# A fused transformer step: the seven products of halves are summed along chains in PSUM instead of on VectorE

## Chip, cores and metric

The kernel runs on one core of a Trainium2 chip. The metric is the device time of one execution in microseconds (us); shorter is better.

## What is computed

One step of a decoder layer for 2048 prompt tokens and 32 sample tokens, 1024 wide: a mixer (gated linear attention beside a spatial gating unit), a cross-attention over 256 memory tokens, and a gated feed-forward part with a causal convolution of width 3 (ConvFFN, 2816 wide). The two places that the change touches are these lines:

```python
q = (hn @ wq_x).reshape(B, T, MEM_HEADS, MEM_DH)
s = jnp.einsum('bthd,bmhd->bhtm', q, mk).astype(jnp.float32) * (MEM_DH ** -0.5)
p = jax.nn.softmax(s, axis=-1).astype(mv.dtype)
...
g = hn @ w_gate
gp = jnp.concatenate([buf.astype(g.dtype), g], axis=1)
c = conv_b + sum(conv_w[j] * gp[:, j:j + T] for j in range(CONV_W))
out = (jax.nn.gelu(c) * (hn @ w_up)) @ w_down
```

## The kernel before

The prompt runs in four blocks of 512 tokens, block 0 to 3; the 32 sample tokens ride along in the mixer of block 1 and in the ConvFFN of block 2, and their own cross-attention is spread over the ConvFFN of block 1 (its matmuls are `sop`, `soT`, `kTp`; its values are loaded as `vc`). Every fp32 product is three matmuls of rounded parts (`mm3`, L91 to L94: high by high, high by low, low by high). ScalarE (ACT) makes a high part and VectorE (DVE) the low one (`split`, L84 and L85).

Gate, up and the scores use a product of 2 x 2 halves with seven products instead of eight. The halves of a weight tile are A11, A12, A22 and the sums S1 to S4; the tokens are cut into halves of H = 256 (272 in block 2, with the sample tokens). One FFN step (`seven_step`) makes 256 columns of gate or up for a block: seven products of 4 x 3 = 12 matmuls. There are 11 gate and 11 up steps in each of the blocks 1 to 3; the very first gate step of each of these blocks takes another path (`early`). A score half-block (`sc{s}{i}`, two per block) is seven products of 24 matmuls. The names read as follows: `wup18S2` is block 1, up, step 8, half S2; `a_...` is the PSUM result, `r_q_...` the tile in SBUF with the four quarters q0 to q3 that the seven results add up to; `h_wup..` and `l_wup..` are the split parts of a loaded sum `r_wup..`. `g`, `c` and `acth` are the gate, its convolution and the product with up, `d` the down product.

Before, each product has a PSUM result of its own. With H = 256 ("joint" steps) S1 and S3 share a bank and S4 and A22 share one, at different columns. ScalarE copies A11 to q0 (L266); VectorE adds the other six results in: L268 (q3 = S2 + q0), L273 (q1 and q2 from S1, S3 and q3 in one instruction), L279 (q3 = S3 + q1), L258 (q0 += A12), L286 (q1 and q2 += S4 and A22); with H = 272 and in the scores each add is an instruction of its own. In the scores the copy is L1325, the adds are L1322, and `soften` (maximum, exponential, sum) follows for each quarter.

A scheduler of the framework sets each engine's order from the program and its own estimates, and takes PSUM results from two pools of four banks, `acc` and `mps`; neighbouring steps are interleaved by it. Accesses of two engines to one bank are kept apart with semaphores by it, whatever columns they touch. Each engine works through its queue strictly in order; the loads are issued from SyncE's queue (SPq). The input of the next block is loaded (L757) while the FFN still runs, and ScalarE squares it (`junk`, L758) for its norm.

## Time and profile before

| | |
|---|---|
| time, median of 3 runs | 2842.79 us (2840.3 to 2844.05) |
| span of the profiled execution | 2835.0 us |
| TensorE (PE) busy | 2794.4 us, 99% |
| VectorE (DVE) busy | 1891.3 us, 67% |
| ScalarE (ACT) busy | 1104.5 us, 39% |
| GpSimd (POOL) busy | 575.5 us, 20% |
| mean granted TensorE clock | 0.996 |
| DMA | 638.21 MB, 225 GB/s |

The span runs from the first to the last instruction of one execution taken with the profiler; the page gives no other time for that execution, and the median of the runs lies 7.8 us above its span. Busy times of different engines overlap. The ConvFFN stretches of the blocks 1, 2 and 3 are 1127 to 1484, 1818 to 2142 and 2483 to 2788 us of the span.

### The profile page before, as it was taken

Reading aid. Unit: us, or ns where it says so; the run is one execution under the profiler, and the core shown is the slowest. Engines: PE = TensorE matmul, PEld = TensorE weight load, DVE = VectorE, ACT = ScalarE, POOL = GpSimd, SP = SyncE. Lnnn points to the kernel's source line nnn. Section 1 sums busy time; section 2 is a strip of 40 time slices with the busy share of each in tenths; the row PEclk is TensorE's granted clock in tenths of the full one; section 3 lists DMA queues with packets and bytes.
Section 4 is the critical chain, followed back from the end, with each engine's and each line's share of the span. In section 5 each row is a group of like instructions: output and inputs, shape, how many; then the busy total and the mean of one; then the engine's idle time right before and its main releaser. Section 6 shows DMA issues by size and latency. Waiting matters only on the chain.

```text
span 2835.0 us, 47063 instructions
## 1 busy us (share of the span) xinstructions
PE 2794.4 (99%) x17894; PEld 2473.9 (87%) x17894; DVE 1891.3 (67%) x3266; ACT 1104.5 (39%) x1950; POOL 575.5 (20%) x638
## 2 busy tenths in 40 slices
PE   8999999999999999999999999999999999999998
PEld 8888888888888898898888889899999888899997
DVE  6578778777657776655555777766666677665555
ACT  5645544333363354222124445422223545421222
POOL 2002212111111221222220121222221022132222
PEclk9999999999999999999999999999999999999999
DMA  9756589999932255888995226577776323577775
GB/s 306 244 182 219 188 273 340 335 339 333 328 109 77 83 164 196 309 290 290 324 340 169 82 61 208 196 260 256 258 264 215 102 70 133 201 260 273 271 282 177
DMA packets 369687, 638.21 MB, mean 225 GB/s; under 512 B 27370, under 2 KB 238412, under 8 KB 369462
## 3 DMA queue, kind: packets, MB, share of 16 engines
q1 hardware_dynamic: 369462, 635.20, 65.9%
q8 instruction: 142, 2.33, 0.3%
q14 instruction: 83, 0.68, 0.1%
HBM read 507.69 MB, written 127.41 MB: 224 GB/s over the span
## 4 chain that ended last, share of the span: by engine, by line
PE 61%; DVE 4%; ACT 1%; issue 1%; POOL 1%; DMA 0%; POOLq 0%; SPq 0%; DVEq 0%; ACTq 0%
PE d L94 4%; PE d L92 4%; PE d L93 4%; PE a_wx L94 1%; PE a_wx L93 1%; PE a_wx L92 1%; PE s L1044 1%; PE a_wo L92 1%; PE a_wo L93 1%; PE a_wu L92 1%; PE a_wu L93 1%; PE a_wo L94 1%; PE t_wr L92 1%; PE t_wr L93 1%; PE a_wu L94 1%
## 5 line engine op out<-in xcount | busy, mean ns | idle before, releaser
L92 PE MATMUL d<-acth,whi_wd 128*128 128x272 f32 (+1 forms) x688 | 235.3, 342 | 0.0
L94 PE MATMUL d<-acth,wlo_wd 128*128 128x272 f32 (+1 forms) x688 | 233.3, 340 | 0.0
L93 PE MATMUL d<-actl,whi_wd 128*128 128x272 f32 (+1 forms) x688 | 233.0, 339 | 0.0
L1679 DVE TENSOR_TENSOR h<-d,h 128x512 f32<-128x512 f32 (+1 forms) x232 | 133.5, 581 | 148.0 <-PE d L94 147.8
L1581 POOL TENSOR_TENSOR c<-c,bc_f 128x512 f32<-128x512 f32 (+1 forms) x88 | 139.3, 1589 | 134.2 <-ACT c L1580 133.4
L1571 ACT ACTIVATE c<-g,colsb 128x512 f32<-128x512 f32 x88 | 71.7, 815 | 202.9 <-DVE g L1540 152.7
L94 PEld LDWEIGHTS d<-acth,wlo_wd 128*128 128x128 f32 x688 | 129.3, 188 | 15.5 <-issue 1.2
L93 PEld LDWEIGHTS d<-actl,whi_wd 128*128 128x128 f32 x688 | 129.3, 188 | 13.6 <-issue 0.4
L92 PEld LDWEIGHTS d<-acth,whi_wd 128*128 128x128 f32 x688 | 129.5, 188 | 13.1
L1603 POOL TENSOR_TENSOR c<-r_q_wup,c 128x512 f32<-128x512 f32 (+1 forms) x33 | 63.0, 1908 | 337.7 <-DVE r_q_wup L286 215.9
L1568 POOL COPY carry<-g 128x2 f32<-128x2 f32 x88 | 30.6, 348 | 432.8 <-DVE g L1540 430.7
L92 PE MATMUL a_wo<-ch,h_wo 128*128 128x512 f32 (+1 forms) x320 | 113.2, 365 | 2.3 <-ACT r L874 1.5
L93 PE MATMUL a_wo<-cl,h_wo 128*128 128x512 f32 (+1 forms) x320 | 113.4, 357 | 0.0
L94 PE MATMUL a_wo<-ch,l_wo 128*128 128x512 f32 (+1 forms) x320 | 112.6, 355 | 0.0
L1572 DVE SCALAR_TENSOR_TENSOR c<-g,colsb,c 128x512 f32<-128x512 f32 x88 | 86.0, 978 | 29.0 <-ACT c L1571 28.3
L84 ACT ACTIVATE acth<-c 128x512 fp32r<-128x512 f32 (+1 forms) x88 | 55.9, 636 | 117.1 <-DVE c L1603 87.3
L94 PE MATMUL a_wx<-pTh,wlo_wx 128*128 128x512 f32 x256 | 101.2, 395 | 0.0
L93 PE MATMUL a_wx<-pTl,whi_wx 128*128 128x512 f32 x256 | 100.5, 393 | 0.0
L92 PE MATMUL a_wx<-pTh,whi_wx 128*128 128x512 f32 x256 | 100.2, 394 | 0.0
L1580 ACT ACTIVATE c<-c 128x512 f32<-128x512 f32 (+1 forms) x88 | 56.1, 637 | 96.6 <-DVE c L1573 84.7
L1573 DVE SCALAR_TENSOR_TENSOR c<-g,colsb,c 128x512 f32<-128x512 f32 x88 | 88.0, 1000 | 1.1
L85 DVE TENSOR_TENSOR actl<-c,acth 128x512 fp32r<-128x512 f32 (+1 forms) x88 | 64.2, 733 | 27.2 <-ACT acth L84 26.2
(3753 smaller groups left out, 9725.5 us busy)
## 6 DMA issues: line engine op xcount, KB each, us to landing
whi_wd<-wd SPq DMA_DIRECT2D x66, 512.0 KB, 7.8
wlo_wd<-wd SPq DMA_DIRECT2D x66, 512.0 KB, 7.5
r_wo<-in_w_out_dram SPq DMA_DIRECT2D x32, 512.0 KB, 3.5
wlo_wx<-vod SPq DMA_DIRECT2D x32, 512.0 KB, 4.1
whi_wx<-vod SPq DMA_DIRECT2D x32, 512.0 KB, 4.8
r_wg<-in_w_gate_dram SPq DMA_DIRECT2D x22, 512.0 KB, 7.4
r_wup<-in_w_up_dram SPq DMA_DIRECT2D x22, 512.0 KB, 4.7
r_wd<-in_w_down_dram SPq DMA_DIRECT2D x22, 512.0 KB, 4.3
```

The source lines that it names most:

```text
L84: act.activation(hi, src, AF.Copy)
L85: (lo_eng or dve).tensor_tensor(lo, src, hi.bitcast(F32), ALU.subtract)
L92: pe.matmul(ps, wh, xh, start=first, stop=False)
L93: pe.matmul(ps, wh, xl, start=False, stop=False)
L94: pe.matmul(ps, wl, xh, start=False, stop=last)
L1571: act.activation(c[:, :SB], g[:, 2:SB + 2], AF.Identity, bias=cb, scale=w2)
L1572: dve.scalar_tensor_tensor(c[:, :SB], g[:, 1:SB + 1], w1, c[:, :SB], ALU.mult, ALU.add)
L1573: dve.scalar_tensor_tensor(c[:, :SB], g[:, 0:SB], w0, c[:, :SB], ALU.mult, ALU.add)
L1580: act.activation(c[:, :T], c[:, :T], AF.Gelu_apprx_tanh)
L1581: pool.tensor_tensor(c[:, :T], c[:, :T], B.fbc[:, :T], ALU.mult)
L1603: (dve, pool)[i].tensor_tensor(c[:, :T], q[i], c[:, :T], ALU.mult)
L1679: dve.tensor_tensor(B.h[m + mm][:, cs], ps[:, :cw], B.h[m + mm][:, cs], ALU.add)
```

## The change

The four chains x (A11, S2, S3), y (S1, S4), z (A12) and w (A22) each get one PSUM result, and a product is added onto its chain by TensorE. The running sums are copied out by ScalarE: A11 to q0, A11+S2 to q1, A22 to q2, S1 to q3. VectorE then adds x onto q2 and q3 once (after S3), and z and y onto q0 and q1 once (after S4). In joint steps x and w share one bank, and z and y another; A22 and A12 start there without the flag that starts a sum, since another sum is open in the bank. The order of products becomes A11, S1, A12, S2, A22, S3, S4. The number of matmuls stays the same. The first gate step of a block (`early`) computes as before.

```diff
@@ mm3
-    def mm3(ps, wh, wl, xh, xl, first, last):
-        pe.matmul(ps, wh, xh, start=first, stop=False)
...
+    def mm3(ps, wh, wl, xh, xl, first, last, again=False):
+        pe.matmul(ps, wh, xh, start=first, stop=False, skip_group_check=again)
...
+    CHAIN = {"A11": "x", "S2": "x", "S3": "x", "S1": "y", "S4": "y", "A12": "z", "A22": "w"}
+    COPIED = {"A11": 0, "S2": 1, "A22": 2, "S1": 3}
@@ seven_step
-        seq = ("A11", "S1", "A12", "S2", "S3", "S4", "A22") if early else ("A11", "S2", "S1", "S3", "A12", "S4", "A22")
-        joint = 2 * H <= 512 and not early
+        seq = ("A11", "S1", "A12", "S2", "S3", "S4", "A22") if early else ("A11", "S1", "A12", "S2", "A22", "S3", "S4")
+        joint = 2 * H <= 512
...
-                if nm == "A11":
-                    act.activation(q0, got(nm), AF.Copy)
-                elif nm == "S2":
-                    dve.tensor_tensor(q3, got(nm), q0, ALU.add)
...
-                elif nm == "S3":
-                    if joint:
-                        dve.tensor_tensor(q[:, H:3 * H].rearrange("p (s t) -> p s t", s=2),
-                                          ps[nm][0].rearrange("p (s t) -> p s t", s=2),
-                                          q3.unsqueeze(1).broadcast_to([128, 2, H]), ALU.add)
-                    else:
-                        dve.tensor_tensor(q1, got("S1"), q3, ALU.add)
-                        dve.tensor_tensor(q2, got(nm), q3, ALU.add)
-                    dve.tensor_tensor(q3, got(nm), q1, ALU.add)
-                elif nm == "A12" and not early:
-                    c11()
-                elif nm == "S4" and not joint:
-                    dve.tensor_tensor(q1, got(nm), q1, ALU.add)
-                elif nm == "A22":
-                    if joint:
-                        dve.tensor_tensor(q[:, H:3 * H], ps[nm][0], q[:, H:3 * H], ALU.add)
-                    else:
-                        dve.tensor_tensor(q2, got(nm), q2, ALU.add)
+                if joint:
+                    xw, zy = acc(f"a_{name}x"), acc(f"a_{name}z")
+                    at_ = {"x": xw[:, :H], "w": xw[:, H:2 * H], "z": zy[:, :H], "y": zy[:, H:2 * H]}
+                else:
+                    at_ = {i: acc(f"a_{name}{i}")[:, :H] for i in "xyzw"}
+                q23 = q[:, 2 * H:4 * H].rearrange("p (s t) -> p s t", s=2)
+                for nm in seq:
+                    i = CHAIN[nm]
+                    fresh = nm in ("A11", "S1") or not joint and nm in ("A12", "A22")
+                    for k in range(last + 1):
+                        mm(at_[i], nm, k, fresh and k == 0, k == last)
+                    if nm in COPIED:
+                        act.activation(q[:, COPIED[nm] * H:(COPIED[nm] + 1) * H], at_[i], AF.Copy)
+                    elif nm == "A12" and not joint:
+                        dve.tensor_tensor(q0, at_["z"], q0, ALU.add)
+                    elif nm == "S3":
+                        dve.tensor_tensor(q23, at_["x"].unsqueeze(1).broadcast_to([128, 2, H]), q23, ALU.add)
+                    elif nm == "S4" and joint:
+                        dve.tensor_tensor(q[:, 0:2 * H], zy[:, 0:2 * H], q[:, 0:2 * H], ALU.add)
+                    elif nm == "S4":
+                        dve.tensor_tensor(q1, at_["y"], q1, ALU.add)
@@ score
-        SEQ = ("A11", "S1", "A12", "S2", "S3", "S4", "A22")
+        SEQ = ("A11", "S1", "A12", "S2", "A22", "S3", "S4")
...
-                ps = B.ps[nm] = acc(f"sc{s}{i}{nm}")
+                fresh = nm in ("A11", "S1", "A12", "A22")
+                if fresh:
+                    B.ps[CHAIN[nm]] = acc(f"sc{s}{i}{nm}")
+                ps = B.ps[CHAIN[nm]]
...
+                if nm in COPIED:
+                    o = COPIED[nm]
+                    q[o] = T_(f"p{s}{i}{o}")
+                    act.activation(q[o][:, :512], ps, AF.Copy)
+                for o in {"A12": (0,), "S3": (3, 2), "S4": (1,)}.get(nm, ()):
+                    dve.tensor_tensor(q[o][:, :512], ps, q[o][:, :512], ALU.add)
+                    soften(i, o)
```

Two places show how the order moves; both are up 8 and gate 9 of block 1 (`wup18`, `wg19`), where the next block's input (`x2_00` and so on) is squared. First ScalarE's queue, before the change (L266 are the copies of A11):

```order
L84 ACTIVATE h_wup18S2_14539<-r_wup18S2_14537 128x1024
L1580 ACTIVATE c117_14653<-c117_14653 128x512
L84 ACTIVATE h_wup18S1_14665<-r_wup18S1_14663 128x1024
L266 ACTIVATE r_q_wup18_14856<-a_wup18A11_14857 128x256
L758 ACTIVATE junk_90,xss2_15569<-x2_00_15579 128x512
L758 ACTIVATE junk_90,xss2_15569<-x2_01_15582 128x512
L84 ACTIVATE h_wup19S2_14973<-r_wup19S2_14971 128x1024
L758 ACTIVATE junk_90,xss2_15569<-x2_10_15585 128x512
L84 ACTIVATE acth116_14953<-c116_14643 128x512
L758 ACTIVATE junk_90,xss2_15569<-x2_11_15588 128x512
L266 ACTIVATE r_q_wg19_14985<-a_wg19A11_14986 128x256
```

And with the change, where the copies have the line L280 (the rows of up 8 are in turn S1, A11+S2 and, behind two squares and an `acth`, A22; those of gate 9 A11 and S1):

```order
L280 ACTIVATE r_q_wup18_14796<-a_wup18z_14798 128x256
L280 ACTIVATE r_q_wup18_14796<-a_wup18x_14797 128x256
L758 ACTIVATE junk_90,xss2_15494<-x2_00_15504 128x512
L84 ACTIVATE acth116_14890<-c116_14583 128x512
L758 ACTIVATE junk_90,xss2_15494<-x2_01_15507 128x512
L280 ACTIVATE r_q_wup18_14796<-a_wup18x_14797 128x256
L758 ACTIVATE junk_90,xss2_15494<-x2_10_15510 128x512
L84 ACTIVATE h_wup19S1_14910<-r_wup19S1_14908 128x1024
L280 ACTIVATE r_q_wg19_14922<-a_wg19x_14923 128x256
L280 ACTIVATE r_q_wg19_14922<-a_wg19z_14924 128x256
L758 ACTIVATE junk_90,xss2_15494<-x2_11_15513 128x512
L280 ACTIVATE r_q_wg19_14922<-a_wg19x_14923 128x256
```

Before, one copy per step stands here, gate 9's behind four squares. Now three copies stand between the squares: up 8's last one behind `x2_01`, gate 9's first two behind `x2_10` and `h_wup19S1`.

Second, TensorE at the end of up 8, before the change (the last matmuls of A22, a step of the sample's output, and gate 9's A11):

```order
L92 MATMUL a_wup18S4_14926<-wuhwx17_11533,wup18A22_14755 128x256
L93 MATMUL a_wup18S4_14926<-wulwx17_11534,wup18A22_14755 128x256
L94 MATMUL a_wup18S4_14926<-wuhwx17_11533,wup18A22_14755 128x256
L1404 MATMUL sop0_14964<-r_so00_14757,sos_14835 32x256 x4
L92 MATMUL a_wg19A11_14986<-w1wx11_11275,wg19A11_14795 128x256
L93 MATMUL a_wg19A11_14986<-w1wx11_11275,wg19A11_14795 128x256
```

And with the change, from the last matmuls of A22 to the first of S3 of up 8 (`h_wup18S1` holds S1 and S3):

```order
L92 MATMUL a_wup18x_14797<-wuhwx17_11521,wup18A22_14695 128x256
L93 MATMUL a_wup18x_14797<-wulwx17_11522,wup18A22_14695 128x256
L94 MATMUL a_wup18x_14797<-wuhwx17_11521,wup18A22_14695 128x256
L1394 MATMUL sop0_14901<-r_so00_14697,sos_14775 32x256 x4
L92 MATMUL a_wg19z_14924<-wthwx17_11512,wg19S1_14782 128x256
L93 MATMUL a_wg19z_14924<-wtlwx17_11513,wg19S1_14782 128x256
L94 MATMUL a_wg19z_14924<-wthwx17_11512,wg19S1_14782 128x256
L1394 MATMUL sop0_14901<-r_so01_14794,sos_14775 32x256 x4
L1394 MATMUL sop0_14901<-r_so10_14899,sos_14775 32x256 x4
L92 MATMUL a_wup18x_14797<-wthwx11_11267,h_wup18S1_14482 128x256
L93 MATMUL a_wup18x_14797<-wtlwx11_11268,h_wup18S1_14482 128x256
L94 MATMUL a_wup18x_14797<-wthwx11_11267,l_wup18S1_14483 128x256
```

Behind A22 came a new step and nothing of up 8 any more; now only the sample's output and the end of gate 9's S1 lie between A22 and S3, which is added onto x in the bank that A22 shares, and so after A22's copy.

More of the change, by code (lines that the diff above doesn't have):

```diff
@@ L89, in split_scaled @@
         dve.scalar_tensor_tensor(lo, src, g, hi.bitcast(F32), ALU.mult, ALU.subtract)
-    def mm3(ps, wh, wl, xh, xl, first, last):
-        pe.matmul(ps, wh, xh, start=first, stop=False)
-        pe.matmul(ps, wh, xl, start=False, stop=False)
-        pe.matmul(ps, wl, xh, start=False, stop=last)
+    def mm3(ps, wh, wl, xh, xl, first, last, again=False):
+        pe.matmul(ps, wh, xh, start=first, stop=False, skip_group_check=again)
+        pe.matmul(ps, wh, xl, start=False, stop=False, skip_group_check=again)
+        pe.matmul(ps, wl, xh, start=False, stop=last, skip_group_check=again)
     def wraw(name):
@@ L240, in fn @@
             q0, q1, q2, q3 = (q[:, i * H:(i + 1) * H] for i in range(4))
-            ps = {}
-            def prod(nm, k0, k1):
-                if nm not in ps:
-                    mate = {"S3": "S1", "A22": "S4"}.get(nm)
-                    if joint and mate:
-                        ps[nm] = ps[mate][0], 1
-                    else:
-                        ps[nm] = (mps if early and len(ps) > 3 else acc)(f"a_{name}{nm}"), 0
-                bank, i = ps[nm]
-                for k in range(k0, k1):
-                    mm3(bank[:, i * H:(i + 1) * H], half(nm, 0, k), half(nm, 1, k), *xs[k][nm], k == 0, k == last)
@@ L254, in got, with mm @@
-            def got(nm):
-                return ps[nm][0][:, ps[nm][1] * H:(ps[nm][1] + 1) * H]
-            def c11():
-                dve.tensor_tensor(q0, got("A12"), q0, ALU.add)
+            def mm(bank, nm, k, first, stop):
+                mm3(bank, half(nm, 0, k), half(nm, 1, k), *xs[k][nm], first, stop, not early)
             if early:
+                ps = {nm: (mps if i > 3 else acc)(f"a_{name}{nm}")[:, :H] for i, nm in enumerate(seq)}
                 for nm in seq:
-                    prod(nm, 0, last)
@@ new lines, in fn @@
+                    for k in range(last):
+                        mm(ps[nm], nm, k, k == 0, False)
+                for nm in seq:
+                    mm(ps[nm], nm, last, False, True)
+                    if nm == "A11":
+                        act.activation(q0, ps[nm], AF.Copy)
+                    elif nm == "S2":
+                        dve.tensor_tensor(q3, ps[nm], q0, ALU.add)
+                        dve.tensor_tensor(q0, ps["A12"], q0, ALU.add)
+                    elif nm == "S3":
+                        dve.tensor_tensor(q1, ps["S1"], q3, ALU.add)
+                        dve.tensor_tensor(q2, ps[nm], q3, ALU.add)
+                        dve.tensor_tensor(q3, ps[nm], q1, ALU.add)
+                    elif nm == "S4":
+                        dve.tensor_tensor(q1, ps[nm], q1, ALU.add)
+                    elif nm == "A22":
+                        dve.tensor_tensor(q2, ps[nm], q2, ALU.add)
+            else:
+                if joint:
+                    xw, zy = acc(f"a_{name}x"), acc(f"a_{name}z")
+                    at_ = {"x": xw[:, :H], "w": xw[:, H:2 * H], "z": zy[:, :H], "y": zy[:, H:2 * H]}
+                else:
+                    at_ = {i: acc(f"a_{name}{i}")[:, :H] for i in "xyzw"}
+                q23 = q[:, 2 * H:4 * H].rearrange("p (s t) -> p s t", s=2)
+                for nm in seq:
+                    i = CHAIN[nm]
[6 more added lines that the diff above has]
+                        dve.tensor_tensor(q0, at_["z"], q0, ALU.add)
+                    elif nm == "S3":
+                        dve.tensor_tensor(q23, at_["x"].unsqueeze(1).broadcast_to([128, 2, H]), q23, ALU.add)
+                    elif nm == "S4" and joint:
+                        dve.tensor_tensor(q[:, 0:2 * H], zy[:, 0:2 * H], q[:, 0:2 * H], ALU.add)
+                    elif nm == "S4":
+                        dve.tensor_tensor(q1, at_["y"], q1, ALU.add)
@@ L1319, in fn @@
                         xh, xl = B.hn[k][nm]
[L1320 removed]
+                        mm3(ps[:, c * 256:(c + 1) * 256], xh[:, cs], xl[:, cs], wh[:, k], wl[:, k],
+                            fresh and c == 0 and k == 0, k == 3, True)
                 q = B.p[i]
[L1322 to L1342 removed]
+                if nm in COPIED:
[5 more added lines that the diff above has]
+                    soften(i, o)
             def load():
```

27 lines of the change are left out of this document (removed).

## Prediction

> **What bounds the kernel now.** I read the page's busy shares first, then a table of the stages that the change touches, then the waits of TensorE.
>
> ```profile
> span 2835.0 us, 47063 instructions
> PE 2794.4 (99%) x17894; PEld 2473.9 (87%) x17894; DVE 1891.3 (67%) x3266; ACT 1104.5 (39%) x1950; POOL 575.5 (20%) x638
> ```
>
> TensorE (PE) is busy for 2794.4 of 2835.0 us, so a time can only fall by fewer or shorter matmuls, or by closing what little idle time there is. The table by stage has, per row, the stretch, its length, the busy time of PE, PEld, DVE, ACT and POOL (instructions in brackets), the granted TensorE clock, the DMA share and GB/s. The first three rows are the ConvFFN of blocks 1, 2 and 3, the next two the scores of blocks 0 and 1.
>
> ```profile
> 1127.00:1484.00 357.00, 356.16 (x2753) 316.91 (x2753) 196.09 (x284) 91.22 (x141) 92.63 (x104) 1.00 0.86 307
> 1818.00:2142.00 324.00, 323.79 (x2582) 323.37 (x2582) 212.50 (x388) 85.52 (x141) 87.61 (x136) 1.00 0.73 258
> 2483.00:2788.00 305.00, 304.74 (x2218) 287.64 (x2218) 177.02 (x261) 74.28 (x111) 83.83 (x88) 1.00 0.77 273
> 324.00:367.00 43.00, 42.90 (x363) 42.70 (x362) 33.22 (x68) 22.63 (x48) 3.87 (x3) 1.00 0.78 265
> 1024.00:1074.00 50.00, 46.81 (x370) 45.38 (x369) 39.35 (x85) 25.69 (x55) 9.24 (x5) 0.97 0.64 218
> ```
>
> In these five stretches TensorE is idle for 0.84, 0.21, 0.26, 0.10 and 3.19 us, 4.6 us together. VectorE (DVE) is busy for 55 to 66% of the FFN stretches and 77 to 79% of the scores; it is not the bound. ScalarE (ACT) is busy for 24 to 26% and 51 to 53%. The waits of TensorE name what ended its idle time (total us, times, longest):
>
> ```profile
> PE otp L1185 <- DVE o L1179: 6.1, 3, 2.9
> PE sc10S L92 <- DVE h L1238: 1.7, 1, 1.7
> PE sop L1495 <- DMA vc<-in_cache_mem_v_dram: 0.5, 1, 0.5
> ```
>
> None of them is an add of a product of halves: the first is in the mixer, the second waits for the normalised input of the scores, the third for sample values from memory. What the change speeds up is therefore not waited for today.
>
> **The change, part by part: matmuls.** Every product keeps its 12 matmuls of 256 columns (272 in block 2) or its 24 in the scores. Adding into a sum that is already in PSUM instead of a fresh result alters only a flag. The first matmuls of two consecutive products of gate 6 in block 3 give the pace:
>
> ```profile
> 2643.83 0.28 PE L92 MATMUL a_wg36A<-w1wx,wg36A 128*128 128x256 f32 x1
> 2644.19 0.28 PE L92 MATMUL a_wg36S<-wuhwx,wg36S 128*128 128x256 f32 x1
> 2645.61 0.28 PE L92 MATMUL a_wg36S<-wthwx,wg36S 128*128 128x256 f32 x1
> ```
>
> From the first row of S2 (2644.19) to the first of S1 (2645.61) are 12 matmuls, 1.42 us, 0.118 us each. All but the first matmul of each product accumulate already, at the same pace. I take 0 us for the flag. No row shows a product that adds onto another product's sum; from the bracketing rows (first matmul of a product and those behind it, both 0.28 us) both ends are 0.
>
> **VectorE.** One gate step of block 1 adds five times now; the scores of one half-block add seven times (count, then duration min/median/max in ns):
>
> ```profile
> L268 DVE TENSOR_TENSOR r_q_wg<-a_wg12S,r_q_wg x1: 417/417/417, 1171.6 to 1171.6; 128x256 f32<-128x256 f32 x1
> L273 DVE TENSOR_TENSOR r_q_wg<-a_wg12S,r_q_wg x1: 692/692/692, 1174.3 to 1174.3; 128x512 f32<-128x512 f32 x1
> L258 DVE TENSOR_TENSOR r_q_wg<-a_wg12A,r_q_wg x1: 425/425/425, 1177.4 to 1177.4; 128x256 f32<-128x256 f32 x1
> L286 DVE TENSOR_TENSOR r_q_wg<-a_wg12S,r_q_wg x1: 692/692/692, 1180.3 to 1180.3; 128x512 f32<-128x512 f32 x1
> L1322 DVE TENSOR_TENSOR p<-sc00S,p x5: 681/683/691, 336.8 to 342.5; 128x512 f32<-128x512 f32 x5
> L1322 DVE TENSOR_TENSOR p<-sc00A,p x2: 681/686/691, 337.5 to 345.5; 128x512 f32<-128x512 f32 x2
> ```
>
> The fifth (L279) has the size of L268. So a joint step costs 3 x 0.42 + 2 x 0.69 = 2.64 us and will cost two adds of 512, 1.38: 1.26 less in each of 42 steps, 53 us. Block 2 goes from seven adds of about 0.43 to two of them and a double one, about 1.4 less in 21 steps, 29 us. Scores lose 3 x 0.69 in 8 half-blocks, 17 us. Some 99 us of VectorE's 1891 go. TensorE waits for none of it, so its worth is bounded by the idle time of the stretches above: 0 to -4.6 us, and the 0.03 of clock that the 50 us scores stretch lacks, 1.5 us. The one big wait there (sc10S, 1.7) is for L1238, ahead of the adds; I take 0.
>
> **ScalarE.** It copies four sums instead of one in 63 FFN steps (three of the 66 copies below belong to the first gate, which stays) and in 8 half-blocks.
>
> ```profile
> 0.00:2835.00 2835.00, 25.46 (x66) 1.00 0.66 225
> L1325 ACT ACTIVATE p<-sc00A x1: 572/572/572, 330.0 to 330.0; 128x512 f32<-128x512 f32 x1
> ```
>
> The first row is ACT's busy time in today's copies (L266): 25.46/66 = 0.386 us each. 189 more cost 73 us, 24 score copies at 0.57 another 14: 87 us on an engine that is busy for 1104.5. That is hidden as work. But a copy is now something that TensorE waits for: S2 may not be added onto A11's bank before A11 is copied out, nor may the other half of that bank be written meanwhile.
>
> The time that a copy has is set by what the order puts between a product and the one that needs its copy. The scheduler interleaves neighbouring steps, so in blocks 1 and 3 this is mostly two products, 2 x 1.42 = 2.8 us, at the tightest usually one (1.42); the scores have at least one product of 24 matmuls, 2.8. In need are 0.39 for the copy plus its start:
>
> ```profile
> 2644.45 0.39 ACT L266 ACTIVATE r_q_wg<-a_wg36A 128x256 f32<-128x256 f32 x1 [4.70 <-PE a_wg36A L94]
> ```
>
> A11's last matmul began just ahead of 2644.19, the copy stood ready and ended at 2644.84. So 0.65 us of 1.42 to 2.8 are used when ScalarE is free, and it may come 0.8 to 2.2 us late at no cost. For this hiding the price is 0 at one end, and at the other the lateness beyond it.
>
> The Trainium skill, "PSUM — Partial Sum Buffer", section "PSUM bank collisions raise a hardware error", speaks against the change: two engines must be kept off a bank as a whole, not off an address in it, so that a copy of one half shuts TensorE out of the other half too. By it each bank has up to four hand-overs a step; this order of products is laid out with such waits, and today's trace, in which no bank changes hands between ScalarE and TensorE within a step, cannot show the price. It is rival two.
>
> **Where ScalarE is late.** ScalarE takes its work strictly in order; what stands ahead of a copy decides. The one place where a slow thing stands there is gate/up 8 and 9 of block 1, in which the squares of the next block's input (`junk`, L758) wait for loads, which wait for the buffers of the last sample values. Today:
>
> ```profile
> 1426.06 1.63 SPq L757 DMA_DIRECT2D x<-in_x_prompt_dram  x3
> 1425.06 0.64 PE L1495 MATMUL sop<-vc,spm 128*32 128x256 f32 x8
> 1426.54 0.64 PE L1495 MATMUL sop<-vc,spm 128*32 128x256 f32 x8 [0.52 <-DMA vc<-in_cache_mem_v_dram]
> 1419.47 1.76 SPq L1437 DMA_DIRECT2D vc<-in_cache_mem_v_dram  x4
> 1434.28 0.64 PE L1404 MATMUL sop<-r_so,sos 128*32 128x256 f32 x8
> 1434.86 0.63 ACT L758 ACTIVATE junk<-x 128x512 bf16<-128x512 f32 x1 [11.08 <-DMA x<-in_x_prompt_dram]
> 1435.61 0.63 ACT L758 ACTIVATE junk<-x 128x512 bf16<-128x512 f32 x1
> 1436.24 1.04 ACT L84 ACTIVATE h_wup19S<-r_wup19S 128x1024 fp32r<-128x1024 f32 x1
> 1438.94 0.36 ACT L266 ACTIVATE r_q_wg<-a_wg19A 128x256 f32<-128x256 f32 x1
> ```
>
> ScalarE stood for 11.08 us, and nobody minded: only gate 9's copy came late, and it has no taker on TensorE. Call T0 the end of the last `sop` (1427.2): the load issues at T0-1.1, the first square starts at T0+7.7. In the new order up 8's copy of A22 stands behind two squares and an `acth`, and S3 of up 8 waits for it. ScalarE: T0+7.7, square 0.75, `acth` 0.53, square 0.63, so the copy runs from T0+9.6 to T0+10.0. TensorE: between T0 and S3 stand 59 matmuls of halves, 7.0 us, and three groups of the sample's output (L1404, 0.57 from the start of one to the next matmul in the trace), 1.7 us, so it is ready at T0+8.7. Stall 1.3. S3 ends near T0+11.4; gate 9's S2 then needs its A11 copy, which stands behind another square and `h_wup19S`: T0+9.9, plus 0.63, plus 1.0, plus 0.39 is T0+11.9, a stall of 0.5. Before that, the last `sop` comes nearer to its load: from the earlier `sop` to it were 5.6 us, in the new order some 4.9, so the 0.52 of waiting becomes about 1.1, 0.6 more. Together 2.4. The ends are 0 (the load lands 2 us sooner) and 5 (2 to 3 us later, with DMA at 86%).
>
> A stall of this size also costs clock. Behind the two long `otp` waits and the sc10S wait the granted clock (third figure from the right) read:
>
> ```profile
> 1026.00:1030.00 4.00, 2.29 (x10) 1.86 (x11) 4.00 (x10) 1.82 (x3) 1.05 (x2) 0.82 0.44 133
> 1030.00:1034.00 4.00, 3.58 (x21) 3.18 (x19) 3.96 (x8) 3.40 (x8) 1.12 (x1) 0.75 0.09 15
> 1684.00:1688.00 4.00, 3.09 (x9) 2.30 (x10) 2.68 (x5) 2.42 (x4) 0.00 (x0) 0.50 0.43 131
> 1688.00:1692.00 4.00, 4.00 (x14) 3.16 (x13) 0.73 (x2) 0.00 (x0) 0.00 (x0) 0.66 0.01 4
> ```
>
> After the 1.7 us wait 4 x 0.18 + 4 x 0.25 = 1.7 us were lost, after the 2.9 us one 4 x 0.50 + 4 x 0.34 = 3.4. I take 1.7, the row nearest to a stall of 1.3; the ends are 0 and 3.4. The Trainium skill, "TensorE: Matmul & The Clock Gate", section "Why this matters for your kernels", would have only gaps over some 3 us lower the clock; the rows above differ with waits of 1.7 and 2.9, and by the page the sum would be 1.7 less.
>
> **Sum.** Matmuls 0, VectorE 0, place at up 8 +2.4, clock +1.7, small lateness of copies elsewhere +0.5 (between 0 and 3; several `h_wup` splits that wait for memory stand ahead of copies in block 1). +4.6 on the span: 2839.6. The three runs' median, 2842.8, lies 7.8 above the profiled span, so 2847.4.
>
> **Rivals.** *One, nothing is felt*: the loads land early enough and all copies stay hidden, 2842 to 2844. For it: only one place has a slow thing ahead. Against it: the 11.08.
>
> *Two, every step stalls*: hand-overs of a bank cost TensorE time even with ScalarE free. If each of 42 joint steps lost 0.65 us once (the copy of gate 6, uncovered), +27; at four times, +109. It decides wherever less than 0.65 us of other products stands in between; against it, the order has 1.42 and more. Likeliest price if it holds in part: 2860 to 2950.
>
> *Three, block 1 stalls at several places*: the splits that wait for memory (`h_wup`) precede copies at gates 1, 7, 10 as well. Today's waits of ScalarE there:
>
> ```profile
> ACT h_wup17S L84 <- DMA r_wup17S<-s7u: 8.1, 1, 8.1
> ```
>
> Two more stalls like the one at up 8, each 1.3 and 1.7 of clock, give +3.0 apiece: one or two of them beside the whole of the forecast, 2850 to 2854, three or four 2856 to 2860.
>
> *Four, faster*: VectorE's 99 us end the scores of block 1 sooner and shift the mixer's work, so that one `otp` wait of 2.9 with its 3.4 us of clock goes: 2843 - 6.3 = 2836.5. It decides once VectorE reaches L1179 3 us sooner; against it, that line belongs to the mixer, ahead of any changed add of its block.
>
> **How the numbers follow.** The forecast, 2845 to 2851, gets 0.42, two thirds of it within 0.2% (5.7 us, about what a measurement of this kernel tells from no change); rival one 0.22; two 0.06; three 0.23; four 0.07. So faster 0.07, same 0.28 + 0.22 = 0.50, slower 0.14 + 0.06 + 0.23 = 0.43. The range 2838 to 2858 leaves out four, two and the tail of three. Without the rare cases it would be 2842 to 2853.
>
> **What would show it.** In the changed trace the waits of TensorE should name one or two `a_wup18x`/`a_wg19x` rows released by ScalarE's copy, 1 to 3 us, with a clock below 1.00 just behind; FFN stretches of blocks 2 and 3 should keep their idle time of 0.2 to 0.3; DVE should read about 1790 and ACT about 1190. Rows such as `a_wg3…x <- ACT` by the dozen would show rival two. It is wrong if the loads of the next input do not land as today, or if ScalarE lags elsewhere by more than 2 us.

## The result, and the profile after

The changed kernel takes 2849.41 us, the median of six runs (2848.23 to 2854.78); the kernel before, in six runs, 2840.27 (2840.04 to 2844.05). The ratio is 1.0036, its 95% interval 1.0026 to 1.0046, which is 7.4 to 13.1 us more. The profiled execution of the changed kernel is the slowest of its six, 2854.78 us, and the one of before a quick one, so the two spans are 18.1 us apart, twice the 9.1 us between the medians; what the waits shown here cost is therefore more than the usual price, and a second profile of the same kernel, at 2849.3 us, stands further below.

The head of the page of the changed kernel:

```profile
span 2853.1 us, 46922 instructions
PE 2801.9 (98%) x17894; PEld 2479.9 (87%) x17894; DVE 1796.5 (63%) x3032; ACT 1181.5 (41%) x2163; POOL 561.7 (20%) x638
```

VectorE lost 95 us of work and ScalarE gained 77. TensorE has the same number of matmuls. The table by stage, with the ConvFFN of blocks 1, 2 and 3 (columns as before):

```profile
1127.00:1490.00 363.00, 354.56 (x2697) 314.34 (x2696) 163.30 (x220) 110.02 (x200) 85.59 (x102) 0.99 0.83 292
1818.00:2160.00 342.00, 341.55 (x2684) 339.58 (x2683) 197.78 (x319) 115.80 (x215) 96.72 (x140) 1.00 0.73 254
2483.00:2808.00 325.00, 322.15 (x2299) 301.64 (x2298) 157.08 (x212) 104.13 (x184) 76.62 (x91) 1.00 0.75 264
```

The idle time of TensorE, length less busy time, is now 8.4 us in block 1 (0.8 before), 0.5 in block 2 (0.2) and 2.9 in block 3 (0.3). The stretches do not hold quite the same work as before: over the whole of block 3, from its gate 0 to the end of the span, the idle time is 12.5 us against 10.5. Even so the loss is in blocks 1 and 3, where two chains share a bank, and not in block 2. Which waits they are, from TensorE's waits (total us, times, longest; rows selected); the first two stand for what the change left as it was:

```profile
PE otp L1185 <- DVE o L1179: 5.9, 3, 2.9
PE sc10S L92 <- DVE h L1238: 1.6, 1, 1.6
...
PE d L92 <- DMA whi_wd<-wd: 6.1, 2, 3.4
PE a_wg36z L92 <- DMA wg36S<-s7g: 0.9, 1, 0.9
PE d L92 <- DVE r_q_wg L286: 0.8, 1, 0.8
PE a_wg11x L92 <- ACT r_q_wg L280: 0.6, 1, 0.6
PE sop L1485 <- DMA vc<-in_cache_mem_v_dram: 0.5, 1, 0.5
PE a_wg34z L92 <- DMA wg34S<-s7g: 0.3, 1, 0.3
PE a_wup18x L92 <- ACT r_q_wup L280: 0.2, 1, 0.2
```

In the changed steps 7.3 us are ended by weight loads (6.1 + 0.9 + 0.3), 0.8 by ScalarE's copies (0.6 + 0.2) and 0.8 by VectorE's add of z and y (L286), which a down product of block 3 waits for. The largest is the first down product (`d`) of a group of hidden columns, waiting for its weights `whi_wd`. The timeline at both places, after the change (start, duration, engine, line; in brackets the idle time before and what ended it; SPq rows are the issue of a load):

```profile
1246.35 0.32 SPq L124 DMA_DIRECT2D whi_wd<-wd  x1
1252.72 0.60 PE L1440 MATMUL kTp<-ident,kc 128*128 128x128 f32 x4
1256.08 0.47 PE L92 MATMUL d<-acth,whi_wd 128*128 128x512 f32 x1 [2.76 <-DMA whi_wd<-wd]
1257.42 0.42 PE L92 MATMUL a_wg14z<-wbhwx,wg14A 128*128 128x256 f32 x1
...
1326.12 0.32 SPq L124 DMA_DIRECT2D whi_wd<-wd  x1
1336.34 0.76 PE L92 MATMUL d<-acth,whi_wd 128*128 128x512 f32 x1 [3.38 <-DMA whi_wd<-wd]
```

And the first of these places before the change:

```profile
1241.40 0.32 SPq L124 DMA_DIRECT2D whi_wd<-wd  x1
1253.44 0.28 PE L94 MATMUL a_wg14S<-wuhwx,wg14A 128*128 128x256 f32 x1
1254.35 0.48 PE L92 MATMUL d<-acth,whi_wd 128*128 128x512 f32 x1
```

Before, gate 4 was finished (the last matmuls of its A22, `wuhwx`), and `d` came behind it, 12.95 us after its load had been issued. Now `d` stands ahead of gate 4's A12 (`a_wg14z`) and all that follows it. From issue to use are 9.73 us here and 10.22 at the second place, but TensorE's waiting is in these: without it (2.76 and 3.38 us) it was ready 6.97 and 6.84 us after the issue, where before it came 12.95 and 11.47 us after. These loads take about 10 us in this stage, as this row of the transfers of before shows (512 KB, median from issue to landing):

```profile
whi_wd<-wd SPq DMA_DIRECT2D x22, 512.0 KB, 10.2
```

So a load that used to land in time with some 1 to 3 us to spare is now asked for 4.6 to 6 us nearer to its use, and is late by up to 3.4. The clock falls with each wait (table of 4 us stretches; the third figure from the right is the granted clock):

```profile
1256.00:1260.00 4.00, 3.92 (x17) 3.68 (x18) 0.00 (x0) 0.00 (x0) 0.00 (x0) 0.58 1.03 412
...
1332.00:1336.00 4.00, 0.95 (x9) 0.75 (x7) 0.89 (x1) 1.42 (x3) 0.74 (x1) 0.89 0.99 363
1336.00:1340.00 4.00, 3.67 (x13) 3.21 (x14) 1.16 (x3) 0.00 (x0) 0.00 (x0) 0.50 1.03 419
1340.00:1344.00 4.00, 4.00 (x28) 4.00 (x28) 0.47 (x1) 0.38 (x1) 0.00 (x0) 0.75 0.88 325
```

That is 4 x 0.42 = 1.7 us and 4 x (0.11 + 0.50 + 0.25) = 3.4 us. Waits and clock at the two places make 2.8 + 3.4 + 1.7 + 3.4 = 11.3 us. Block 1 as a whole (from the first matmul of its gate 0 to the first of block 2's scores, so with the mixer of block 2) went from 601.5 to 612.2 us, 10.7 more.

### The profile page after: what moved, and what is told of

Its sections match the earlier page's. It is cut to its first block, busy times and chain, and to the rows that moved or that the text cites. A ratio compares the mean times of both kernels' runs of the same rounds, so it can differ in the third digit from the quotient of the medians.

```text
span 2853.1 us, 46922 instructions
## 1 busy us (share of the span) xinstructions
PE 2801.9 (98%) x17894; PEld 2479.9 (87%) x17894; DVE 1796.5 (63%) x3032; ACT 1181.5 (41%) x2163; POOL 561.7 (20%) x638
## 4 chain that ended last, share of the span: by engine, by line
PE 62%; DMA 2%; DVE 2%; ACT 1%; POOL 1%; issue 1%; SPq 0%; POOLq 0%; ACTq 0%; DVEq 0%
PE d L92 4%; PE d L93 4%; PE d L94 4%; PE a_wx L92 1%; PE a_wx L94 1%; PE a_wx L93 1%; PE a_wo L92 1%; PE a_wo L93 1%; PE a_wo L94 1%; PE s L1044 1%; DMA whi_wd<-wd 1%; PE a_wu L92 1%; PE a_wu L93 1%; PE t_wr L92 1%; PE a_wu L94 1%; PE t_wr L93 1%
## 5 line engine op out<-in xcount | busy, mean ns | idle before, releaser
L1571 POOL TENSOR_TENSOR c<-c,bc_f 128x512 f32<-128x512 f32 (+1 forms) x88 | 129.9, 1478 | 148.8 <-ACT c L1570 148.4
L1593 POOL TENSOR_TENSOR c<-r_q_wup,c 128x512 f32<-128x512 f32 (+1 forms) x33 | 47.0, 1425 | 386.8 <-DVE r_q_wup L284 369.1
L1562 DVE SCALAR_TENSOR_TENSOR c<-g,colsb,c 128x512 f32<-128x512 f32 x88 | 71.9, 818 | 49.0 <-ACT c L1561 48.8
L92 PEld LDWEIGHTS a_wo<-ch,h_wo 128*128 128x128 f32 x320 | 61.3, 195 | 12.9 <-ACT r L874 2.3
```

What stands on the lines that cost most here:

```text
L92: pe.matmul(ps, wh, xh, start=first, stop=False, skip_group_check=again)
L1562: dve.scalar_tensor_tensor(c[:, :SB], g[:, 1:SB + 1], w1, c[:, :SB], ALU.mult, ALU.add)
L1571: pool.tensor_tensor(c[:, :T], c[:, :T], B.fbc[:, :T], ALU.mult)
L1593: (dve, pool)[i].tensor_tensor(c[:, :T], q[i], c[:, :T], ALU.mult)
```

## The experiments

Two theories stand against each other. **A**: weights come late. The new order runs A11 and the first down products ahead of their loads, and TensorE waits for memory. **B**: each hand-over between TensorE and ScalarE costs time, since a product added onto a chain must wait for the copy of the sum before it.

The stage lengths of all profiled executions are read as above, from the first matmuls of each stage in the trace (us). "Scores 0" is the time until block 0's scores begin, ahead of everything that the change touches; block 2 runs from its scores to those of block 3, and block 3 from its gate 0 to the end. The medians stand beside those of the kernel before on the same chip.

| run | median / before | ratio (95%) | scores 0 | block 1 | block 2 | block 3 |
|---|---|---|---|---|---|---|
| before | 2840.27 | | 323.9 | 601.5 | 665.3 | 358.5 |
| after | 2849.41 / 2840.27 | 1.0036 (1.0026 to 1.0046) | 328.2 | 612.2 | 665.3 | 363.1 |
| scores and block 2 | 2837.84 / 2838.97 | 0.999 (0.9981 to 0.9999) | 330.5 | 599.8 | 665.2 | 359.0 |
| block 1 | 2853.13 / 2838.97 | 1.0038 (1.0024 to 1.0052) | 326.8 | 612.2 | 664.8 | 360.3 |
| block 3 | 2843.37 / 2838.97 | 1.0013 (1.0004 to 1.0022) | 328.8 | 600.5 | 665.2 | 362.7 |
| down loads early | 2852.82 / 2838.97 | 1.0045 (1.0032 to 1.0057) | 328.1 | 604.8 | 669.6 | 362.8 |
| the same, block 1 only | 2849.08 / 2838.85 | 1.0038 (1.0025 to 1.005) | 327.0 | 606.2 | 665.6 | 363.5 |
| ... and S4 ahead of S3 | 2850.06 / 2838.85 | 1.0033 (1.0021 to 1.0046) | 327.3 | 604.6 | 664.5 | 361.4 |
| copies twice | 2864.05 / 2838.85 | 1.0092 (1.0078 to 1.0106) | 328.6 | 606.6 | 663.1 | 379.9 |
| before, down loads late | 2863.78 / 2838.85 | 1.0095 (1.0079 to 1.011) | 326.5 | 626.3 | 662.5 | 360.3 |
| after, once more | 2851.9 / 2839.69 | 1.0044 (1.0032 to 1.0057) | 329.7 | 604.7 | 665.4 | 362.9 |
| after, six weight buffers | 2887.15 / 2839.69 | 1.0168 (1.0154 to 1.0182) | 342.5 | 612.8 | 676.2 | 363.6 |
| before, six weight buffers | 2886.66 / 2839.69 | 1.0164 (1.0151 to 1.0178) | 344.8 | 609.8 | 676.0 | 361.8 |
| four banks | 2840.66 / 2840.19 | 1.0006 (0.9997 to 1.0015) | 327.8 | 601.4 | 665.5 | 359.4 |

### Where the loss lies: the change in parts

Three kernels take only a part of the change: the scores and the FFN of block 2, the FFN of block 1, the FFN of block 3. In the rest `seven_old`, the step of before, is used. The edit of the first, against the changed kernel (the second has `blk in (1,)`, the third `blk in (3,)`, both with `s in ()`):

```diff
-    def seven_step(plain, sums, get_xs, H, use, name, early=False):
+    def seven_new(plain, sums, get_xs, H, use, name, early=False):
...
+    def seven_step(plain, sums, get_xs, H, use, name, early=False):
+        blk = int(name[2] if name.startswith("wg") else name[3])
+        return (seven_new if early or blk in (2,) else seven_old)(plain, sums, get_xs, H, use, name, early)
...
+        newsc = s in (0, 1, 2, 3)
+        SEQ = ("A11", "S1", "A12", "S2", "A22", "S3", "S4") if newsc else ("A11", "S1", "A12", "S2", "S3", "S4", "A22")
```

> The change only in the scores and in the ConvFFN of block 2 (272 columns, a bank of its own per chain); the joint steps of blocks 1 and 3 as before. Theory A (weights come late: the new order in the joint steps brings the first down matmuls and the A11 products closer behind their loads, so TensorE waits for DMA): the cost sits in blocks 1 and 3, so this kernel is within 3 us of before (2837 to 2844 where before is 2840). Theory B (each hand-over of a sum from TensorE to ScalarE and back costs time): 29 of the 71 changed steps are here, so +3 to +5 us. VectorE busy falls by some 45 us in both.

> The change only in the ConvFFN of block 1. Theory A: most of the loss is here, +4 to +8 us over before, with waits of TensorE named 'd <- DMA whi_wd' of 2 us and more in total and a granted clock below 1.00 behind them. Theory B: 21 of 71 changed steps, +2 to +3 us, and the waits name ScalarE's copies (L280 of the changed kernel).

> The change only in the ConvFFN of block 3, where no sample work shares the DMA queues. Theory A: loads have the same short lead but land sooner, so +1 to +4 us, in waits for wg3.S and wd loads of under 1 us each, without a clock dip. Theory B: as block 1, +2 to +3 us, in waits for ScalarE.

The scores and block 2 cost nothing: 2837.84 against 2838.97 us, with an interval that just leaves out 1 (VectorE's busy time fell by 34 us, where 45 were expected). There, too, four copies a step are made and every chain is handed over; only the banks are not shared. Block 1 alone gives about the whole of the loss, 14 us by its medians and 7 to 15 by the interval of its ratio, more than the 4 to 8 of theory A; block 3 alone gives 4.4. The waits of TensorE with block 1 alone:

```profile
PE d L92 <- DMA whi_wd<-wd: 5.8, 2, 3.4
PE a_wup18x L92 <- ACT r_q_wup L280: 0.9, 1, 0.9
```

Those with block 3 alone:

```profile
PE a_wg34z L92 <- DMA wg34S<-s7g: 1.4, 1, 1.4
PE a_wg36z L92 <- DMA wg36S<-s7g: 0.5, 1, 0.5
```

Both name loads first. In block 1 copies account for 1.3 us of waiting (0.9 at up 8, 0.4 at gate 1) against 5.8 for down weights, with the clock at 0.83 and 0.75 behind the first of these and 0.64 and 0.93 behind the second.

### Loading the down weights earlier

The first pair of down weights of each group is asked for three loads earlier; the rest is the changed kernel.

```diff
         queue = [(i, u) for i, st in enumerate(steps) for u in st.units]
+        for p in range(len(queue)):
+            if getattr(queue[p][1], "early", 0):
+                queue.insert(p - 3, queue.pop(p))
...
+            if s:
+                unit = wready(wdd[f0, m], name)
+                unit.early = m == 0
+                return Step(fn, [unit])
```

> The whole change, and the first pair of down weights of each group of four is loaded three loads earlier (ahead of A22, S3 and S4 of the gate step before it); nothing else is edited. Theory A: the waits 'd <- DMA whi_wd' (6.1 us in the changed kernel) and the clock dips behind them go, so +0 to +5 us over before instead of +9. Theory B: no difference to the changed kernel, +8 to +10 us.

The waits for `whi_wd` fell as A says, from 6.1 to 0.7 us, and block 1 from 612.2 to 604.8; but the unaltered kernel has 604.7 there in its second profile, so this gain is not shown to come from the edit. The time did not fall: 2852.82 us, 13.9 over before, where A gave 0 to 5 and B 8 to 10. TensorE's waits say where it went:

```profile
PE d L92 <- DMA whi_wd<-wd: 0.7, 2, 0.5
PE xt L779 <- ACT sdo L1419: 3.2, 1, 3.2
PE a_wg26w L92 <- DMA wg26A<-w7g: 1.3, 1, 1.3
PE a_wg26y L92 <- DMA wg26S<-s7g: 1.2, 1, 1.2
```

In block 2 the loads that now stand behind the early ones are late (block 2 +4.3 us), and in block 1 the transposes of the next input (`xt`) fell into the place behind the sample's output and wait 3.2 us for it. So the edit was made for block 1 alone:

```diff
+                unit.early = s == 1 and m == 0
```

> As the fourth kernel (whole change, first pair of down weights of each group loaded three loads earlier), but in block 1 alone, so that the loads of block 2 and 3 keep their order. Theory A (weights come late): block 1 loses its two waits for down weights and their clock dips (10.7 us from gate 0 of block 1 to the scores of block 2 in the changed kernel against before, 3.4 in the fourth kernel), block 2 is back at +0, block 3 stays at +4 to +5. Sum +4 to +8 us over before, some 5 us faster than the changed kernel. Theory B (hand-overs between TensorE and ScalarE): no difference to the changed kernel, +9 to +11.

Block 2 is back at 665.6, `whi_wd` is waited for 0.2 us in all, and block 1 stands at 606.2. What is left there is the wait of `xt` for `sdo`, 3.2 us once, as in the row above, with a clock of 0.68 and 0.89 behind it (1.7 us), and 1.1 us for copies (gates 9 and 1).

The total is that of the changed kernel, 2849.08, 10.2 over before: the number that B gave, and A's 4 to 8 was missed. That the stated wait goes and the time stays shows that the late load is not a number that can be subtracted: the order is worked out anew with each edit, and TensorE, busy for 98%, meets another late thing a little further on.

The last of this kind names S4 ahead of S3 too, since in block 3 it is the loads of the sums that are late.

```diff
-        seq = (... ("A11", "S1", "A12", "S2", "A22", "S3", "S4")
+        seq = (... ("A11", "S1", "A12", "S2", "A22", "S4", "S3")
```

> As the kernel before it, and the program names S4 ahead of S3 in the FFN steps, in which order TensorE runs them anyway in blocks 2 and 3. Theory A: S4's weights, with which block 3 waits for memory (0.9 and 0.3 us in the changed kernel, 1.4 and 0.5 with block 3 alone), are asked for earlier, so block 3 falls from +4.5 to +1 to +3 us, the whole to +1 to +6. Theory B: no difference to the changed kernel.

Its five runs lie between 2844.42 and 2853.2 us; the median is 11.2 over before, so A's 1 to 6 was missed. The profile is of the 2844.42, and the same 3.2 us of `xt` are in it. Block 3 lost 2.9 us there instead of 5.0, the direction of A. On the total it decides nothing.

### Is it the copies?

Every copy of a sum in the 63 FFN steps is made twice, 252 copies in each of the two lines.

```diff
                         act.activation(q[:, COPIED[nm] * H:(COPIED[nm] + 1) * H], at_[i], AF.Copy)
+                        act.activation(q[:, COPIED[nm] * H:(COPIED[nm] + 1) * H], at_[i], AF.Copy)
```

> The changed kernel with each of ScalarE's copies in the 63 changed FFN steps done twice, one behind the other (252 more copies of 0.39 us, 98 us of ScalarE). Theory A: other products stand between a copy and its taker, so the copies' length is hidden; within 5 us of the changed kernel either way, by whatever the new order does to the loads. Theory B: the doubled copy is paid at each hand-over, at least once a step: 63 x 0.39 = +25 us over the changed kernel, up to four times that.

It came out at 2864.05 us, 25.2 over before. That is 13 to 16 more than the changed kernel (12.2 and 9.1 over before in its two measurements), between the two expectations, so neither had the size. The 252 copies added 96 us to ScalarE and some 0.06 us each to the time. Of the waits:

```profile
PE a_wup37x L92 <- DMA wup37A<-w7u: 3.6, 1, 3.6
...
PE a_wg19x L92 <- ACT r_q_wg L281: 0.8, 1, 0.8
```

With every copy twice as long, copies end 1.1 us of TensorE's waiting (0.8 here and 0.3 at gate 9 of block 3). Loads end the rest, for the most part those of A11 (`x`) in block 3, which is 21 us longer than before, while block 1, at 606.6, lies between the changed kernel's two profiles (612.2 and 604.7). The order says why block 3 takes it so badly: A11 of up 1, 3, 5 and 7 finds TensorE ready 3.7 to 4.1 us after its load was issued, where it was 8.6 to 10.0 with the change and 11.1 before, and these four wait 9.2 us together. That speaks for A in kind: TensorE ran into its loads and not into its copies. That the scheduler moved A11 forward because it had more time to fill behind a sum is likely, but not shown.

### Is a late load enough?

The kernel before, with block 1's first down pair of each group asked for two pairs later, and no other change:

```diff
+        for p in reversed(range(len(queue))):
+            if getattr(queue[p][1], "late", 0):
+                queue.insert(p + 2, queue.pop(p))
...
+                unit.late = s == 1 and m == 0
```

> The kernel before, unchanged but that in block 1 the first pair of down weights of each group of four is asked for two pairs later (behind those of the next two down steps). No copy and no product is touched. Theory A: the lead of that load over its first matmul falls from 13 to 6 or 8 us where a load takes 10, so TensorE waits 2 to 4 us at several of the six groups, with clock dips behind them: +8 to +30 us over before, waits named 'd <- DMA whi_wd'. Theory B: a lead of some microseconds less is hidden and the time stays within 3 us of before.

Late loads make the kernel before slower, by 25 us, and block 1 by 24.8. But the order of the sample's work moved with the edit, and its waits (`sop`, `sqf`, and 2.4 us of `xt` for `sdo`) come to 10.7 us, more than the 5.7 of the one that was meant:

```profile
PE d L92 <- DMA whi_wd<-wd: 5.7, 2, 3.1
PE sop L1498 <- POOL spm L1391: 4.4, 1, 4.4
PE sqf L1416 <- DVE sqt L1411: 3.9, 1, 3.9
```

So the 25 us are not the price of late weights alone. The first row is what bears on A: it is close to that of the changed kernel (6.1, 2, 3.4), here without any chain and with one copy a step. At its two places TensorE was ready 6.70 and 7.05 us after the issue, and 6.97 and 6.84 in the changed kernel: the same lead makes the same wait, whichever way the steps are summed.

### The changed kernel once more

Nothing is edited. The question is what of the waits comes back.

> The changed kernel unaltered, for a second trace and as the control of the next two. Theory A (weights come late): the same two waits 'd <- DMA whi_wd' in block 1, 2 to 4 us each, and +9 to +11 us over before. Were these waits a chance of the first trace, they would be absent here.

```profile
PE d L92 <- DMA whi_wd<-wd: 1.9, 2, 1.7
PE sop L1485 <- DMA vc<-in_cache_mem_v_dram: 2.0, 2, 1.1
PE d L92 <- DVE kT L1446: 1.3, 1, 1.3
```

This profile is of a run of 2849.3 us (the median of its five is 2851.9, that of the first measurement 2849.41). The down weights are waited for 1.9 us instead of 6.1, and block 1 is 3.2 us over before instead of 10.7; 1.7 and 0.2 of the 1.9 are in blocks 1 and 3. The two places in block 1 are the same, and their loads are issued at 1248.63 and 1324.75:

```profile
1256.95 0.47 PE L92 MATMUL d<-acth,whi_wd 128*128 128x512 f32 x1 [1.34 <-DVE kT L1446]
1333.28 0.47 PE L92 MATMUL d<-acth,whi_wd 128*128 128x512 f32 x1 [1.68 <-DMA whi_wd<-wd]
```

At the first, the row names VectorE's `kT`, which ends at 1256.95; in the trace the load lands at 1256.81, so the two are 0.14 us apart. Counted as above, TensorE was ready 6.98 and 6.85 us after the issue, as in the first profile to 0.01 us. What differs is the load: in the trace it landed 8.2 and 8.4 us after its issue here, and 9.6 and 10.1 there. So the order fixes the lead, the run decides the load, and the wait is the difference.

In this run the loss is spread: from gate 0 of block 1 to its last down product are 406.5 us (400.9 before, 412.9 in the first profile, 401.8 with the four banks of the last experiment), with 3.0 us at these two places, 1.5 more than before for `vc`, and 0.6 for copies; block 3 is 4.4 over before. The clock stayed at 1.00 in the whole of block 1.

### Six weight buffers

If loads are late because buffers come free late, another weight buffer should help the changed kernel more than the one before. Both got one, for one less of three other kinds:

```diff
-NU, NT, NRAW, NW = 49, 6, 5, 5
+NU, NT, NRAW, NW = 48, 5, 4, 6
```

> The changed kernel with six buffers for weights in place of five (one buffer less for token tiles, raw weights and intermediate tiles, to make room). Theory A: each load can be asked for one buffer earlier, so the waits 'd <- DMA whi_wd' and for wg3.S go, and what remains against the next kernel is +0 to +4 us. Theory B (hand-overs): still +8 to +11 us over the next kernel.

> The kernel before with the same buffers as the kernel ahead of it. It hardly waits for weights, so within 4 us of before; it is what the kernel ahead of it is held against.

2887.15 and 2886.66 us: the difference between the two kernels is gone (0.5 us), and so are the waits for `whi_wd`. But both are 47 us slower, from waits that the missing buffers make elsewhere, and by stage block 1 is still 3.0 and block 3 1.8 us longer with the change, made up for by 7.3 us in other stages (2.3 ahead of the scores of block 0, 3.6 from there to block 1, 1.4 from the scores of block 3 to its gate 0). The direction is A's; as a test it is weak.

### A bank for each chain

The last experiment keeps chains, copies, order of products and adds, and takes away only the sharing of banks: blocks 1 and 3 do as block 2 does, with four banks a step (and three adds instead of two).

```diff
-        joint = 2 * H <= 512
+        joint = False
```

> The whole change, but in blocks 1 and 3 each chain has a bank of its own (four banks a step and three adds, as block 2 has it already) in place of two shared ones. A step then fills the pool of four banks, and the order runs a step to its end before the next one's A11 or a down product starts, as in the kernel before; the copies of ScalarE stay, four a step. Theory A (weights come late, because two free banks let the order pull A11 and down products ahead of their loads): the waits 'd <- DMA whi_wd' and for wg3.S go, blocks 1 and 3 return to within 1.5 us of before each, and the whole is within 4 us of before (2837 to 2844 where before is 2840). Theory B (hand-overs of a sum between TensorE and ScalarE cost time): the hand-overs of the three chains are all still there, though none any more for the other half of a bank; half the loss or more stays, +5 to +10 us.

The loss is gone: 2840.66 against 2840.19 us, ratio 1.0006 (0.9997 to 1.0015), block 1 at 601.4 and block 3 at 359.4. ScalarE is as busy as in the changed kernel, with the same copies:

```profile
PE 2798.3 (99%) x17894; PEld 2476.5 (87%) x17894; DVE 1827.0 (64%) x3074; ACT 1181.1 (42%) x2163; POOL 571.6 (20%) x638
```

At the place of the first wait the old order of the work is back:

```profile
1245.65 0.32 SPq L124 DMA_DIRECT2D whi_wd<-wd  x1
1258.27 0.60 PE L1440 MATMUL kTp<-ident,kc 128*128 128x128 f32 x4
1258.62 0.48 PE L92 MATMUL d<-acth,whi_wd 128*128 128x512 f32 x1
```

Gate 4 is done before `d`, and 12.97 us lie between the issue and the use (12.95 before the change, 6.97 with it until TensorE was ready). At the second place they are 9.84 (11.47 and 6.84), and nothing waits for `whi_wd`. So the copies by themselves are not the price. What shared banks do is this: a joint step now takes two banks of the pool `acc` for its whole length, where it took five results, one after another, from the same four. Two banks stay free, and the scheduler fills the time between a sum and its copy with what else could start: the next step's A11 and the first down product. Their loads wait for weight buffers and are issued no earlier, so they lose the 1 to 3 us they had in hand. That the free banks are what lets TensorE run ahead is worked out from the code and not shown by a run; the runs show that without sharing the time is that of before, with the old order and lead at the first place and most of the lead at the second. Four banks also take away the copy of one half shutting out the other, so this run alone does not part A from B. The names of the waits do in block 1 (in the first profile, all blocks together, 7.3 us for loads against 0.8 for copies and 0.8 for VectorE's add), and so do the leads, which are 6.7 to 7.1 us in every profile with these waits. In block 3 the account stays open in part, as told below.

## Why the prediction was right, and where not

The time on record, 2847.4, lies 2.0 us under the measured 2849.41, inside the range. Against the six runs of before the change cost 9.1 us, twice the 4.6 of the sum, and it is slower by more than the 0.2% bound, which the prediction held a little less likely (0.43) than no change (0.50). That the total came so near is luck for the most part: the forecast stood on a median of three runs, 2842.79, that is 2.5 us over that of six; of its terms +2.4, +1.7 and +0.5 the first profile shows 0.2, 0 and 0.6; and the largest part of the loss was not in the sum at all.

**Right: matmuls, VectorE, ScalarE's work.** The flag costs nothing (scores and block 2, with the new chains, 0.999). VectorE reads 1796.5 (about 1790 forecast) and ScalarE 1181.5 (about 1190); its 252 copies at L280 take 96.56 us, 0.383 us each (0.386 taken). VectorE's relief brought 1 us at most where part of it could be seen alone (scores and block 2): the long `otp` waits are 5.9 us (6.1), sc10S 1.6 (1.7). Rival four is refuted. Rival two, that every step stalls, as well: the copies of 42 joint steps are waited for 0.8 us in all, where one uncovered copy a step would have made 27. The rule of bank sharing in the Trainium skill, "PSUM — Partial Sum Buffer", section "PSUM bank collisions raise a hardware error", that a bank is guarded as a whole and not by address, is what the order keeps to: S3 of up 8 starts behind the copy of A22, which lies in the other half of its bank (last row below). Its price as a wait for copies is those 0.8 us; what it costs through the order is the rest of this account.

**Mis-sized: up 8 and gate 9, +2.4 and clock +1.7.** The step that was worked out at length went as it was told, with a tenth of the price. The rows there:

```profile
1443.98 2.22 SPq L757 DMA_DIRECT2D x<-in_x_prompt_dram  x4
1443.32 0.64 PE L1485 MATMUL sop<-vc,spm 128*32 128x256 f32 x8 [0.51 <-DMA vc<-in_cache_mem_v_dram]
1444.32 0.64 PE L1485 MATMUL sop<-vc,spm 128*32 128x256 f32 x8
1452.17 0.63 ACT L758 ACTIVATE junk<-x 128x512 bf16<-128x512 f32 x1 [3.97 <-DMA x<-in_x_prompt_dram]
1453.93 0.36 ACT L280 ACTIVATE r_q_wup<-a_wup18x 128x256 f32<-128x256 f32 x1
1454.34 0.39 PE L92 MATMUL a_wup18x<-wthwx,h_wup18S 128*128 128x256 f32 x1 [0.22 <-ACT r_q_wup L280]
```

With T0 = 1445.0 the first square starts at T0+7.2 (7.7 forecast), the copy at T0+9.0 (9.6), and TensorE comes to S3 at T0+9.1 (8.7). The load was 0.5 us sooner and TensorE 0.4 later, and of a stall of 1.3 us 0.2 was left, since the copy was done 0.7 us sooner than forecast; gate 9 did not wait at all (0.5 forecast). The `sop` waits 0.51, as before (0.6 more forecast). So 0.2 us instead of 2.4, and no dip of the clock. In the second profile the `sop` waits 1.5 us longer than before and up 8 again 0.2, so 1.7, also at full clock. The difference of two sums of 9 us, each known to half a microsecond, cannot carry a stall of 1.3.

**Missing: the lead of the weights.** The largest part of the loss came from a term that is not in the sum: 11.3 us at two places in the first profile, and in the second 3.0 beside the 4.4 of block 3. The prediction asked what stands ahead of a copy on ScalarE; it did not ask what the scheduler moves forward on TensorE when a step leaves two banks free, nor how much lead the loads of that work had. Nearest was rival three (block 1 stalls at several places for memory, each with its clock, 2850 to 2860), but it put the stalls on ScalarE, behind the splits that wait for memory; they are on TensorE itself. The "small lateness of copies elsewhere, +0.5" is right for the copies (0.6 at gate 1) and stood for too little. The sign that block 3 would keep its idle time failed: 4.6 us are lost there, 2.0 of them idle, in the waits `a_wg36z` and `a_wg34z` for loads (1.2) and of `d` for VectorE's add (0.8). The other 2.6 are in no wait: TensorE is busy for 350.7 us over the stage instead of 348.0, and what lengthened it is not shown (with four banks, 348.9). Of 150 loads of gate, up and down weights there, 27 are used less than 9 us after their issue (the least 5.7), and before 1 was (8.99); with four banks it is 11 (the least 7.6) and the stage is back at 359.4.

**The rest of the 18.1 us.** Of the difference of the two profiled spans, block 1 holds 10.7, block 3 4.6 and block 0 4.3, the rest -1.5. The 4.3 lie ahead of the first changed instruction, and the other profiles have between 326.5 and 330.5 us there with the buffers as they were, the kernel before with its late loads among them (326.5), against 323.9 in the profile of before. They are not a cost of the change.

## What to carry to other kernels

Ask of a change to accumulators not only what it waits for but what it lets run ahead: buffers set free on one side (here two PSUM banks) move work forward until it meets a limit on the other side (here weights that are still loading). Read for each load how long it is in flight and how long before its use it is issued; a lead of 13 us for a load of 10 is a margin of 3, and an edit that pulls its use forward by 6 makes a wait of 3. Take the waiting itself off the lead that a trace shows, or a late load looks nearly in time. Here, with TensorE busy for 98%, relief of VectorE was worth 1 us at most, and repairing a single late load showed the next one: the repair that worked here took away the cause (the sharing of banks), not the waits.

## What the runs showed of the hardware

**Clock behind short waits.** Waits of 2.8 and 3.4 us for weights cost 1.7 and 3.4 us of clock on top. Even shorter ones can: ahead of block 0's scores both kernels have the same two waits (`otp` for `vol`, 2.2 us together, the longest 1.3). In the profile of before, the clock stays at 1.00 there in every stretch of 4 us from 276 to 304; in that of the changed kernel it does not:

```profile
288.00:292.00 4.00, 1.83 (x9) 1.21 (x10) 3.08 (x5) 0.68 (x3) 1.91 (x1) 0.83 0.98 336
292.00:296.00 4.00, 3.86 (x11) 2.79 (x10) 2.73 (x4) 2.37 (x4) 0.00 (x0) 0.50 0.76 278
296.00:300.00 4.00, 4.00 (x16) 3.20 (x15) 0.00 (x0) 0.00 (x0) 0.00 (x0) 0.81 0.00 0
```

4 x (0.17 + 0.50 + 0.19) = 3.4 us, in work that the change does not touch. The Trainium skill, "TensorE: Matmul & The Clock Gate", section "Why this matters for your kernels", asks for no idle gap over some 3 us; here the clock fell behind a gap of 2.8 (to 0.58) and around gaps of 1.3, in one execution and not in another, so a shorter gap is no assurance. Nor is the price of a gap fixed: the one `otp` wait of 2.8 us in the mixer of block 2 cost 3.4 us of clock in the profile of before (the rows 0.50 and 0.66 of the prediction), 1.7 in the first profile of the change (one stretch at 0.57) and nothing in the second, where the clock reads 1.00 from 1676 to 1712 around it.

**Loads of one program land differently in each execution.** The same order of the same program, with the same leads, waited 6.1 us at two down loads in one profile and 3.0 in the next, because the loads landed 9.6 and 10.1 us after their issue in the one and 8.2 and 8.4 in the other. A margin of a few us per load is used up in some runs and not in others, and a single profile of a kernel without that margin may tell a bad or a good case, here 10.7 or 3.2 us of block 1.
